# Twelve weight pieces of layer 1: the low part formed by a negation and an accumulating DMA in place of a subtraction on VectorE

## The chip, the cores and the metric

The kernel runs on one core of one Trainium2 chip. The metric is the device time of one execution in microseconds; the median of 3 runs of the kernel before is 1392.16 us (1390.02 to 1392.28).

## The reference

Two layers of a gated block on 512 tokens with 1024 channels, all in float32. What matters of it:

```python
for i in range(DEPTH):                                   # 2 layers
    xn = rmsnorm(x, norm1_g[i])
    proj = xn @ w_in[i]
    u_pool, q, k, v, g_a, g_b = jnp.split(proj, splits, axis=-1)
    ...                                                  # 4 heads, two q/k pairs of 128 each, v of 256
    q = apply_partial_rotary(rmsnorm(q, q_norm_g[i]), cos, sin)     # k the same
    o = diff_attention(q, k, v, lam)                     # softmax(q0 k0) - lam * softmax(q1 k1), chunk-causal, times v
    o = rmsnorm(o, subln_g[i]) * (1.0 - lam_init)
    pool_out = pool_mixer(u_pool, pool_w[i], pool_scale[i])
    merged = sigmoid(g_a) * pool_out + sigmoid(g_b) * o
    x = x + merged @ w_out[i]
    gate, up = jnp.split(rmsnorm(x, norm2_g[i]) @ w_ffn_in[i], 2, axis=-1)
    x = x + (silu(gate) * up) @ w_ffn_out[i]
```

## The kernel before

**Products in three parts.** Every float32 operand is split into a high part, rounded to the type that TensorE multiplies (fp32r), and a low part, the remainder. A product is then three matmuls into the same accumulator: high by high, high by low, low by high (`product`, `three`, `in_turn`; lines 271 to 273 and 290 to 292).

**Weights.** They come from HBM in 243 pieces of 128 x 1024 floats (512 KB, two rows of 128 channels by 512 columns) in the order of a list. `loaded` issues a piece's load on SyncE's queue into one of 7 `raw` buffers. `parts` makes its two parts in one of 6 pairs of buffers (`whi`, `wlo`). It has two forms:

- Without a piece number it calls `split` (line 201): ScalarE copies the piece into `whi`, and VectorE subtracts that from the piece into `wlo`.
- With a piece number (lines 225 to 227) ScalarE copies the piece into `whi` and writes the negated piece into `wlo` (an activation with scale -1), and GpSimd issues a DMA from the weights in HBM that adds the piece to `wlo` as it lands, so that the remainder is left. The DMA waits for the negation, and for this form a piece is read from HBM twice. 64 pieces take it, all of them in the feed-forward parts.

`wblock` gives the four pieces of one block of `w_in` for one head (1024 channels by 512 columns), all by the first form. A head has three such blocks: q/k, v with one gate, and u with the other gate.

**Order of the heads.** The heads are taken in the order 3, 2, 1, 0 (`ORDER`). `attention(j, before, then)` computes a head's q and k for four blocks of 128 tokens (each: 24 matmuls, an eviction with squares on ScalarE, the norm and the rotation on VectorE), then v and a gate. After q and k of the next head's second block, `then` computes the previous head's u and gate part (`merged`). The list of loads has the same order: q/k of a head, its v/gate, and then the u/gate of the head before.

**Work between the matmuls.** Scores, softmax, the product with v and the norm behind it are put into a heap with a due time (`later`), and taken out between the matmuls of other products when a count of TensorE's columns (`clock`) has passed it (`run_due`). So TensorE's order is: some weights' matmuls, then the scores of one block, and so on.

**Transposes through HBM.** In all heads but the first of layer 0, q and k, the probabilities and the attention's output are transposed by `turned` (lines 300 to 320): VectorE transposes in 32 x 32 squares into `near` (line 305), SyncE's queue writes `near` to HBM (`away`) and reads it back in four pieces (line 310). Then ScalarE casts the result to its high part (`qh`, or `ah` for the probabilities) and VectorE subtracts the low part (`ql`, `al`), both with line 201. Scores are lines 505 to 525, the casts and the product with v lines 538 to 558.

**GpSimd** does two things here: the power of -1/2 of the norms (`r`, line 335), in between VectorE's sums and its scaling (line 589), and the issuing of the accumulating DMAs (line 227), both in one queue in the order of the program. Also on ScalarE's queue is a DMA: the load of the pooling weights (`pwr`, line 638), into one of the same 7 `raw` buffers.

Of the kernel before, what the change touches and what calls it, by code (L numbers as in the profile page):

```python
# [23 lines left out]
KD = D // P  # L24
# [26 lines left out]
ORDER = (3, 2, 1, 0)  # L51
# [72 lines left out]
def trunk_kernel(  # L124
# [16 lines left out]
    def mm_ps():  # L141
        return ps.tile([P, 512], F32, name="mm", tag="mm", bufs=6)
# [60 lines left out]
    def split_half(hi, lo, src):  # L203

        half = nc.scalar.activation(hi, src, AF.Copy, scale=0.5)
        return half, nc.vector.scalar_tensor_tensor(lo, src, 0.5, hi.bitcast(F32), op0=ALU.mult, op1=ALU.subtract)

    def loaded():

        i = at[0]  # L210
        at[0] += 1
        raw = sb.tile([P, 2, 512], F32, name="raw", tag="raw", bufs=RAWS)
        transfers.append(nc.sync.dma_start(raw.rearrange("p a b -> p (a b)"), wts[i]))
        return raw, i
# [3 lines left out]
    def parts(raw, piece_no=None):  # L218

        hi = sb.tile([P, 2, 512], F32R, name="whi", tag="whi", bufs=SPLITS)  # L220
        lo = sb.tile([P, 2, 512], F32R, name="wlo", tag="wlo", bufs=SPLITS)
        if piece_no is None:
            made[:] = split(hi, lo, raw)
        else:
            nc.scalar.copy(hi, raw)
            made[0] = nc.scalar.activation(lo, raw, AF.Copy, scale=-1.0)  # L226
            nc.gpsimd.dma_start(lo.rearrange("p a b -> p (a b)"), wts[piece_no], accum_op=ALU.add)  # L227
        return hi, lo

    def rows_of(pair, n=2):  # L230

        hi, lo = (x.rearrange("p a b -> p (a b)").rearrange("p (k c) -> p k c", k=n) for x in pair)
        return [(hi[:, k, :], lo[:, k, :]) for k in range(n)]

    def piece(n=2, by_dma=False):
        raw, i = loaded()
        return rows_of(parts(raw, i if by_dma else None), n)

    def wblock(n):

        return [pair for _ in range(n // 2) for pair in piece()]


    clock = [0]
# [40 lines left out]
    def product(acc, pairs):  # L285

        n = len(pairs)
        for i, ((ah, al), (bh, bl)) in enumerate(pairs):
            run_due()
            nc.tensor.matmul(acc, lhsT=ah, rhs=bh, start=i == 0, stop=False)  # L290
            nc.tensor.matmul(acc, lhsT=ah, rhs=bl, start=False, stop=False)  # L291
            last = nc.tensor.matmul(acc, lhsT=al, rhs=bh, start=False, stop=i == n - 1)  # L292
            clock[0] += 3 * acc.shape[-1]
        return last
# [48 lines left out]
    def need(*keys):  # L343
        run_due(lambda: all(k in ready for k in keys))
# [9 lines left out]
    def pair(name, tag, n):  # L354
        return [sb.tile([P, n, S], F32R, name=name + part, tag=tag, bufs=2) for part in "hl"]
# [117 lines left out]
    for layer in range(L):  # L473
# [8 lines left out]
        def x_all(t0=0, t1=NT):  # L482
            return [(xh[:, k, t0 * P:t1 * P], xl[:, k, t0 * P:t1 * P]) for k in range(KD)]

        def cut(pairs, c0, c1):
            return [(h[:, c0:c1], l[:, c0:c1]) for h, l in pairs]

        def attention(j, before, then):

            if before is not None:  # L490
# [84 lines left out]

            at_start = not layer and j == ORDER[0]
            if not at_start:
                w = wblock(KD)
            held = []

            def evicted(t, acc):
# [33 lines left out]
                need(*((layer, before, "o", t) for t in range(NT)))  # L615
            vh, vl = pair("v", "v", 2)
            tb = [sb.tile([P, 2, VD], F32, name="tb", tag="tb", bufs=2) for _ in range(2)]
            w = wblock(KD)
            if at_start:
                with tc.issue_after(transfers[-1].ins):  # L620
                    for i in range(L):
# [14 lines left out]
        def pool_weights(j):  # L636
            raw = sb.tile([P, 2, VD], F32, name="pwr", tag="raw", bufs=RAWS)
            nc.scalar.dma_start(raw.rearrange("p a b -> p (a b)"), pool_w[layer, j])
            both = sb.tile([P, 2, 2, VD], F32R, name="pw", tag="pw")
            hi, lo = both[:, 0], both[:, 1]  # L640
            split(hi, lo, raw)
            return [(hi[:, a, :], lo[:, a, :]) for a in range(2)]

        def windowed(j, c, acc, uh, ul):

            window = WINDOWS[j]
            up = sb.tile([P, 16 + S], F32, name="up", tag="up", bufs=2)
            nc.vector.memset(up[:, :16], 0.0)
            nc.vector.tensor_mul(up[:, 16:], acc, rms_rows[layer])
            prev, step, n = up, 1, 0  # L650
            while step < window:
                cur = sb.tile([P, 16 + S], F32, name="us", tag="us", bufs=2)
                nc.vector.memset(cur[:, :16], 0.0)
                nc.vector.tensor_add(cur[:, 16:], prev[:, 16:], prev[:, 16 - step:16 + S - step])
                prev, step, n = cur, step * 2, n + 1
            head = sb.tile([P, 16], F32, name="head", tag="head", bufs=2)
            nc.vector.tensor_mul(head, prev[:, 16:32], inv_t[:, j, :])
            nc.vector.scalar_tensor_tensor(
                prev[:, 32:], prev[:, 32:], 1.0 / window, up[:, 32:], op0=ALU.mult, op1=ALU.subtract)
            nc.vector.tensor_sub(prev[:, 16:32], head, up[:, 16:32])  # L660
            split(uh[:, c, :], ul[:, c, :], prev[:, 16:])

        def merged(j, mj, mh, ml):

            w = wblock(KD)
            pw = pool_weights(j)
            uh, ul = pair("u", "u", 2)
            for c in range(2):
                acc = mm_ps()
                product(acc, list(zip(cut(w, c * P, (c + 1) * P), x_all())))  # L670
                windowed(j, c, acc, uh, ul)

            gates = []
            for c in range(2):
                acc = mm_ps()
                product(acc, list(zip(cut(w, VD + c * P, VD + (c + 1) * P), x_all())))
                ta = sb.tile([P, S], F32, name="ta", tag="ta", bufs=2)
                nc.vector.tensor_mul(ta, acc, rms_rows[layer])
                nc.scalar.activation(ta, ta, AF.Tanh, scale=0.5)
                gates.append(ta)  # L680
            need(*((layer, j, "mj", t) for t in range(NT)))
            for c in range(2):
                y = mm_ps()
                product(y, list(zip(cut(pw, c * P, (c + 1) * P), [(uh[:, a, :], ul[:, a, :]) for a in range(2)])))
                ta = gates[c]
                k = KD * layer + 2 * j + c
                nc.vector.scalar_tensor_tensor(ta, ta, 1.0, y, op0=ALU.add, op1=ALU.mult)
                nc.vector.scalar_tensor_tensor(ta, ta, scale[:, k:k + 1], mj[:, c, :], op0=ALU.mult, op1=ALU.add)
                split_half(mh[:, c, :], ml[:, c, :], ta)
# [257 lines left out]
        def mix(i):  # L947
            j = ORDER[i]
            if i == 2:
                need(*((layer, ORDER[3], "s", t) for t in range(NT)))  # L950
                ms[j] = pair("m", "qk", 4)
            else:
                ms[j] = pair("m", "m", 2)
            merged(j, mjs[j], *ms[j])

        for i, j in enumerate(ORDER):
            then = (lambda: project_out(ORDER[i - 2])) if i >= 2 else None
            mjs[j] = attention(j, ORDER[i - 1] if i else None, then)
            if i:
                mix(i - 1)  # L960
# [68 lines left out]
```

## Time and profile before

| | |
|---|---|
| median of 3 runs | 1392.16 us (1392.28, 1390.02, 1392.16) |
| profiled execution, its own time | 1391.49 us |
| its span in the profile | 1389.7 us |
| TensorE busy | 1375.8 us, 99% |
| VectorE busy | 1042.5 us, 75% |
| ScalarE busy | 704.1 us, 51% |
| GpSimd busy | 118.2 us, 9% |
| mean granted TensorE clock | 0.997 |
| weight pieces made by an accumulating DMA | 64 of 243 |

How to read it: the span is the time between the first and the last instruction that the profiler saw; the execution's own time is 1.8 us longer. Layer 1 begins at about 690 us in this profile. A line such as L201 is line 201 of the kernel; PE is TensorE, DVE VectorE, ACT ScalarE, POOL GpSimd, SP SyncE. In a timeline each row has the start in us, the length in us, the engine, the line, the operation, output<-inputs, and in brackets the idle time before it and what ended it.

### The profile page before, as it was taken

How to read it: one execution, taken by the hardware profiler on the slowest of the kernel's cores; microseconds unless marked ns; L12 is line 12 of the kernel's file. 1: busy time of each engine (PE TensorE's matmuls, PEld its weight loads, DVE VectorE, ACT ScalarE, POOL GpSimd, SP SyncE). 2: the span in 40 equal slices, each digit the busy share in tenths (PEclk: the TensorE clock that was granted, in tenths of full speed). 3: DMA queues.
4: the chain of work that ended last, by engine and by line, in shares of the span. 5: the costliest groups of instructions: out<-in, count | busy, mean ns of one | idle time of the engine just before them, and what ended most of it. 6: DMA issues, size and time to landing. Idle time of an engine off the chain costs nothing.

```text
span 1389.7 us, 18568 instructions
## 1 busy us (share of the span) xinstructions
PE 1375.8 (99%) x6242; PEld 1142.0 (82%) x6242; DVE 1042.5 (75%) x1979; ACT 704.1 (51%) x1321; POOL 118.2 (9%) x139
## 2 busy tenths in 40 slices
PE   9999999999999999999999889999999999999999
PEld 7888888888888888888888778888888888888887
DVE  7778778786869768578667787786868686785782
ACT  7545353454766545564435443444547565554540
POOL 1010100000111001110011100000001010011100
PEclk9999999999999999999999999999999999999999
DMA  8333454444667868686334345534446688687741
GB/s 311 104 124 112 147 162 131 148 136 134 152 181 191 240 177 225 164 208 209 109 121 137 106 135 165 163 122 148 140 129 151 183 199 220 195 219 173 199 129 61
DMA packets 141071, 224.52 MB, mean 162 GB/s; under 512 B 40880, under 2 KB 88496, under 8 KB 140976
## 3 DMA queue, kind: packets, MB, share of 16 engines
q1 hardware_dynamic: 130464, 187.65, 42.1%
q0 software_dynamic: 9216, 33.56, 13.8%
q10 hardware_dynamic: 1296, 2.12, 0.5%
q8 instruction: 49, 0.80, 0.2%
q14 instruction: 46, 0.38, 0.1%
HBM read 194.04 MB, written 29.23 MB: 161 GB/s over the span
## 4 chain that ended last, share of the span: by engine, by line
PE 93%; DVE 3%; issue 1%; DMA 1%; POOL 1%; ACT 0%; SPq 0%; DVEq 0%; POOLq 0%; ACTq 0%
PE mm L272 14%; PE mm L273 14%; PE mm L271 14%; PE mm L292 13%; PE mm L290 13%; PE mm L291 13%; PE sc L271 3%; PE sc L273 3%; PE sc L272 3%; PE sc L291 1%; PE sc L292 1%; PE sc L290 1%; DVE qn L589 1%; POOL r L335 1%; DVE wlo L201 1%
## 5 line engine op out<-in xcount | busy, mean ns | idle before, releaser
L201 DVE TENSOR_TENSOR wlo<-raw,whi 128x1024 fp32r<-128x1024 f32 (+1 forms) x221 | 266.7, 1211 | 62.9 <-ACT whi L201 62.3
L201 ACT CAST whi<-raw 128x1024 fp32r<-128x1024 f32 (+1 forms) x221 | 229.9, 1047 | 165.0 <-PE mm L273 60.3
L290 PE MATMUL mm<-whi,xh 128*128 128x512 f32 x480 | 189.0, 394 | 0.0
L291 PE MATMUL mm<-wlo,xh 128*128 128x512 f32 x480 | 187.5, 391 | 0.0
L292 PE MATMUL mm<-whi,xl 128*128 128x512 f32 x480 | 187.3, 390 | 0.0
L273 PE MATMUL mm<-fh,wlo 128*128 128x512 f32 (+1 forms) x356 | 137.8, 387 | 0.0
L272 PE MATMUL mm<-fl,whi 128*128 128x512 f32 (+1 forms) x356 | 137.8, 387 | 0.0
L271 PE MATMUL mm<-fh,whi 128*128 128x512 f32 (+1 forms) x356 | 137.8, 387 | 0.0
L692 DVE TENSOR_TENSOR res<-mm,res 128x512 f32<-128x512 f32 (+1 forms) x145 | 98.1, 680 | 43.1 <-PE mm L273 41.8
L292 PEld LDWEIGHTS mm<-whi,xl 128*128 128x128 f32 x480 | 90.3, 188 | 19.2
L290 PEld LDWEIGHTS mm<-whi,xh 128*128 128x128 f32 x480 | 90.4, 188 | 17.4
L291 PEld LDWEIGHTS mm<-wlo,xh 128*128 128x128 f32 x480 | 90.5, 188 | 17.2
L227 POOL DMA_DIRECT2D wlo<-in_wts x64 | 56.1, 877 | 536.8 <-ACT wlo L226 364.1
L335 POOL TENSOR_TENSOR r<-r,mhalf 128x1 f32<-128x1 f32 (+1 forms) x64 | 56.4, 882 | 528.8 <-DVE r L334 509.0
L291 PE MATMUL mm<-xl,whi 128*128 128x512 f32 x256 | 100.4, 392 | 0.0
L290 PE MATMUL mm<-xh,whi 128*128 128x512 f32 x256 | 100.3, 392 | 0.0
L292 PE MATMUL mm<-xh,wlo 128*128 128x512 f32 x256 | 100.0, 391 | 0.0
L273 PE MATMUL mm<-whi,xl 128*128 128x512 f32 x224 | 87.2, 389 | 0.0
L271 PE MATMUL mm<-whi,xh 128*128 128x512 f32 x224 | 87.2, 389 | 0.0
L272 PE MATMUL mm<-wlo,xh 128*128 128x512 f32 x224 | 87.2, 389 | 0.0
L226 ACT ACTIVATE wlo<-raw 128x1024 fp32r<-128x1024 f32 x64 | 67.7, 1057 | 29.0 <-PE mm L272 27.3
L271 PEld LDWEIGHTS mm<-fh,whi 128*128 128x128 f32 x356 | 66.9, 188 | 13.6
(217 smaller groups left out, 2939.4 us busy)
## 6 DMA issues: line engine op xcount, KB each, us to landing
raw<-in_wts SPq DMA_DIRECT2D x243, 512.0 KB, 3.9
wlo<-in_wts POOLq DMA_DIRECT2D x64, 512.0 KB, 6.1
away<-near SPq DMA_DIRECT2D x72, 256.0 KB, 2.4
near<-away SPq DMA_DIRECT2D x288, 64.0 KB, 2.5
away<-near SPq DMA_DIRECT2D x28, 128.0 KB, 1.7
near<-away SPq DMA_DIRECT2D x112, 32.0 KB, 2.5
pwr<-in_pool_w ACTq DMA_DIRECT2D x8, 256.0 KB, 2.7
away<-pr SPq DMA_DIRECT2D x7, 256.0 KB, 2.0
```

The source lines that it names most:

```text
L201: return nc.scalar.copy(hi, src), nc.vector.tensor_sub(lo, src, hi.bitcast(F32))
L226: made[0] = nc.scalar.activation(lo, raw, AF.Copy, scale=-1.0)
L227: nc.gpsimd.dma_start(lo.rearrange("p a b -> p (a b)"), wts[piece_no], accum_op=ALU.add)
L271: nc.tensor.matmul(acc, lhsT=ah, rhs=bh, start=start, stop=False, **check)
L272: nc.tensor.matmul(acc, lhsT=ah, rhs=bl, start=False, stop=False, **check)
L273: last = nc.tensor.matmul(acc, lhsT=al, rhs=bh, start=False, stop=stop, **check)
L290: nc.tensor.matmul(acc, lhsT=ah, rhs=bh, start=i == 0, stop=False)
L291: nc.tensor.matmul(acc, lhsT=ah, rhs=bl, start=False, stop=False)
L292: last = nc.tensor.matmul(acc, lhsT=al, rhs=bh, start=False, stop=i == n - 1)
L335: nc.gpsimd.tensor_tensor(r, r, mhalf[:, :width], op=ALU.pow)
L589: nc.vector.scalar_tensor_tensor(qn[:, h, :], acc[:, h * QK:(h + 1) * QK], r[:, h:h + 1], g, op0=ALU.mult, op1=ALU.mult)
L692: return nc.vector.tensor_add(res[d][:, cs], acc, res[d][:, cs])
```

## The change

`wblock` takes a number of pieces that are to be made by the second form. In layer 1, for the first two heads of the order (3 and 2), and for each of their three blocks, that is two of four: the first two pieces. So twelve pieces, two heads by three blocks by two, are made by a copy and a negation on ScalarE and an accumulating DMA that GpSimd issues, where they were made by a copy on ScalarE and a subtraction on VectorE. Nothing else is changed in the code.

```diff
-    def wblock(n):
-
-        return [pair for _ in range(n // 2) for pair in piece()]
+    def wblock(n, by_dma=0):
+
+        return [pair for i in range(n // 2) for pair in piece(2, i < by_dma)]
...
+        def by_dma(j):
+            return 2 if layer and j in ORDER[:2] else 0
+
         def attention(j, before, then):
...
-                w = wblock(KD)
+                w = wblock(KD, by_dma(j))
...
             tb = [sb.tile([P, 2, VD], F32, name="tb", tag="tb", bufs=2) for _ in range(2)]
-            w = wblock(KD)
+            w = wblock(KD, by_dma(j))
...
         def merged(j, mj, mh, ml):

-            w = wblock(KD)
+            w = wblock(KD, by_dma(j))
```

The compiler's scheduler places the instructions on each engine by the costs that it assumes, so the order changes as well. Lines behind line 487 have numbers that are larger by 3 in the changed kernel. Three places:

VectorE at head 3's third block of q and k, in layer 1: `r` is the norm's factor, `qn` the scaled q and k, `m` the rotation, `wlo` the weights of head 2's q/k block, `ql` the low part of an earlier block, and `near` the square transpose that begins the trip through HBM. Before:

```order
L334 TENSOR_SCALAR r<-ss_6696,stats 128x2 x2
L589 SCALAR_TENSOR_TENSOR qn<-mm,r,hg 128x128 x4
L201 TENSOR_TENSOR wlo<-raw,whi 128x1024
L362 TENSOR_TENSOR m_6709<-qn,tab 128x128
L366 TENSOR_TENSOR m_6709<-qn,tab 128x4x16 x2
L201 TENSOR_TENSOR wlo<-raw,whi 128x1024
L367 TENSOR_TENSOR qn<-m_6709 128x4x32
L201 TENSOR_TENSOR ql<-near,qh 128x4x128
L201 TENSOR_TENSOR wlo<-raw,whi 128x1024
L305 STREAM_TRANSPOSE near<-qn 128x4x4x32
```

And now:

```order
L334 TENSOR_SCALAR r<-ss_6698,stats 128x2 x2
L592 SCALAR_TENSOR_TENSOR qn<-mm,r,hg 128x128 x4
L201 TENSOR_TENSOR wlo<-raw,whi 128x1024
L362 TENSOR_TENSOR m_6711<-qn,tab 128x128
L366 TENSOR_TENSOR m_6711<-qn,tab 128x4x16 x2
L201 TENSOR_TENSOR ql<-near,qh 128x4x128
L367 TENSOR_TENSOR qn<-m_6711 128x4x32
L305 STREAM_TRANSPOSE near<-qn 128x4x4x32
```

The two subtractions on either side of `qn` and `ql` are gone, and `ql` stands one place earlier.

ScalarE where head 3's scores of its third block (`pr`, 384 columns) are made and head 2's v/gate weights are split; `vh` and `tb` are evictions of head 3's v and gate, `pwr` is the load of the pooling weights. Before:

```order
L201 CAST whi<-raw 128x1024 x2
L627 ACTIVATE vh<-mm,stats 128x256
L201 CAST whi<-raw 128x1024
L201 CAST ah<-pr 128x128
L630 ACTIVATE tb<-mm,stats 128x256
L520 ACTIVATE pr,st<-sc,mx 128x384 x2
L638 DMA pwr<-in_pool_w 128x512
```

And now:

```order
L201 CAST whi<-raw 128x1024
L225 CAST whi<-raw 128x1024
L226 ACTIVATE wlo<-raw 128x1024
L630 ACTIVATE vh<-mm,stats 128x256
L201 CAST ah<-pr 128x128
L225 CAST whi<-raw 128x1024
L523 ACTIVATE pr,st<-sc,mx 128x384 x2
L633 ACTIVATE tb<-mm,stats 128x256
L226 ACTIVATE wlo<-raw 128x1024
L641 DMA pwr<-in_pool_w 128x512
```

Two negations have come in, one of them directly ahead of the load of `pwr`, and `tb` stands behind `pr` now.

GpSimd from the end of layer 0 through the heads of layer 1; the rows with a minus are before, those with a plus now, and `r` is the power of the norms:

```order
-L227 DMA wlo<-in_wts 128x1024 x26
+L227 DMA wlo<-in_wts 128x1024 x30
 L416 TENSOR_TENSOR stats<-stats,mhalf 128x4
-L335 TENSOR_TENSOR r<-r,mhalf 128x4 x6
+L335 TENSOR_TENSOR r<-r,mhalf 128x4 x3
+L227 DMA wlo<-in_wts 128x1024 x2
+L335 TENSOR_TENSOR r<-r,mhalf 128x4
+L227 DMA wlo<-in_wts 128x1024 x2
+L335 TENSOR_TENSOR r<-r,mhalf 128x4 x2
```

Four of the twelve issues stand before layer 1's first norm of q and k, and of the next four two stand ahead of the power for head 3's fourth block, two ahead of those for head 2's first and second block.

TensorE's order is the same but for two matmuls of head 2's first q/k block, which stand behind the six matmuls of head 3's last scores (512 columns) instead of ahead of them.

## The prediction

> **What bounds the kernel now.** I read the page first: the engines' shares, and the DMA queues.
>
> ```profile
> PE 1375.8 (99%) x6242; PEld 1142.0 (82%) x6242; DVE 1042.5 (75%) x1979; ACT 704.1 (51%) x1321; POOL 118.2 (9%) x139
> ...
> q1 hardware_dynamic: 130464, 187.65, 42.1%
> q0 software_dynamic: 9216, 33.56, 13.8%
> ```
>
> TensorE is busy for 1375.8 of 1389.7 us. VectorE, which the change relieves, has a quarter of its time free. So a subtraction less is worth something only where TensorE waits for VectorE, and all of TensorE's idle time is 1389.7 - 1375.8 = 13.9 us. The waits of TensorE say where the largest pieces are:
>
> ```profile
> PE mm L290 <- ACT ah L201: 6.4, 2, 3.2
> PE sc L290 <- ACT pr L520: 0.9, 1, 0.9
> ```
>
> The columns are the total, the count and the longest. TensorE's timeline then dates the waits in layer 1's first heads (the bracket is the idle time before the row, and what ended it):
>
> ```profile
> 732.39 0.39 PE L290 MATMUL sc<-qh 128*128 128x256 f32 x1 [0.86 <-ACT pr L520]
> 769.60 0.39 PE L290 MATMUL mm<-vh,ah 128*128 128x256 f32 x1 [3.24 <-ACT ah L201]
> 790.91 0.44 PE L291 MATMUL sc<-ql,qh 128*128 128x384 f32 x1 [0.54 <-DVE ql L201]
> 820.61 0.39 PE L290 MATMUL mm<-vh,ah 128*128 128x256 f32 x1 [3.15 <-ACT ah L201]
> 821.51 0.39 PE L292 MATMUL mm<-vh,al 128*128 128x256 f32 x1 [0.40 <-DVE up L648]
> ```
>
> I number them: stall 0 (0.86), stall 1 (3.24), stall 2 (0.54), stall 3 (3.15 and 0.40), 8.19 us together. The windows behind stalls 1 and 3 show a second loss. The column after POOL is the granted clock:
>
> ```profile
> 770.60:774.00 3.40, 3.34 (x13) 2.96 (x13) 3.37 (x5) 0.00 (x0) 0.00 (x0) 0.50 0.15 48
> 821.60:825.10 3.50, 3.50 (x13) 3.01 (x14) 1.43 (x5) 0.51 (x3) 0.54 (x1) 0.53 0.55 142
> ```
>
> At half clock, 3.4 us of work take the place of 1.7, so each spell loses about 1.7 us. With 8.2 + 3.4 = 11.6 us the most that this stage can give back is 0.8% of the time. Everything depends on which stalls the removed subtractions stand in front of.
>
> The row behind stall 3 has the clock at 0.53 after a gap of 3.15 us. "TensorE: Matmul & The Clock Gate" of the Trainium skill (Part 1, on the HAM clock gate) lets the clock fall to one half after an idle window of about 3.4 us, in windows that run free of the program. The trace differs in the figure: gaps of 3.24 and 3.15 us were enough here.
>
> **The change part by part.** Twelve weight pieces (4 each for q/k, v/gate and u/gate, in two heads' worth: 2 x 3 x 2) change from a VectorE subtraction to a ScalarE negation plus an accumulating DMA. The prices of one of each:
>
> ```profile
> L201 DVE TENSOR_TENSOR wlo<-raw,whi 128x1024 fp32r<-128x1024 f32 (+1 forms) x221 | 266.7, 1211 | 62.9 <-ACT whi L201 62.3
> ...
> L227 POOL DMA_DIRECT2D wlo<-in_wts x64 | 56.1, 877 | 536.8 <-ACT wlo L226 364.1
> ...
> L226 ACT ACTIVATE wlo<-raw 128x1024 fp32r<-128x1024 f32 x64 | 67.7, 1057 | 29.0 <-PE mm L272 27.3
> ...
> wlo<-in_wts POOLq DMA_DIRECT2D x64, 512.0 KB, 6.1
> ```
>
> VectorE loses 12 x 1.21 = 14.5 us; ScalarE gains 12 x 1.06 = 12.7 us; GpSimd 12 x 0.88 = 10.5 us of issuing. Of the DMA engines, the 64 accumulating transfers on q0 took 13.8% of 1389.7 us, which is 3.0 us of all sixteen engines for each, so 36 us more. These are sums beside TensorE; what counts is their place. Four of the twelve (head 3's q/k and v/gate) are formed before 705 us, where TensorE doesn't wait; two (head 2's u/gate) lie behind 830 us, where it doesn't wait either. I cost these six at nothing: what hides them is the stretch of matmuls with no gap around them, and a landing of 6.1 us that is late by 1 or 2 us would show as a gap of that size. Six are left: head 2's q/k at 719 to 722 us, its v/gate at 738 to 744, head 3's u/gate at 771 to 773.
>
> *Stall 0, head 2's q/k pieces.* The chain of waits that ends at 732.39, in order of time (start, length, what):
>
> ```profile
> 719.06 0.27 DVE m L366 x2
> 719.33 0.10 DVE wlo L201
> ...
> 720.38 0.29 DVE qn L367
> 720.67 0.60 DVE ql L201
> 721.27 1.14 DVE wlo L201
> 722.41 0.63 DVE near L305
> 723.04 0.02 issue
> 723.05 2.15 DMA away<-near
> ...
> 726.60 3.04 DMA near<-away
> ...
> 729.96 0.61 ACT qh L201
> ...
> 730.59 1.28 ACT L520
> ...
> 731.88 0.47 ACT pr L520 x2
> ```
>
> Both subtractions in it go. From the end of m at 719.33, qn (0.29) and ql (0.60) then lead to near at about 720.3, so the round trip through HBM starts 2.1 us earlier. Against that, the two accumulating DMAs are issued at about 718 and 721 (I place them behind the negations on ScalarE), so up to 6.0 us of sixteen engines fall where the engines are needed for the trip and the raw loads. Before, the DMA share (the column before the last) is this:
>
> ```profile
> 724.00:726.00 2.00, 2.00 (x11) 1.65 (x10) 0.58 (x3) 1.08 (x4) 1.01 (x1) 1.00 1.01 300
> 726.00:728.00 2.00, 2.00 (x10) 1.66 (x9) 2.00 (x9) 0.80 (x2) 0.00 (x0) 1.00 0.99 375
> ```
>
> The engines are full there already. The trip (723.05 to 729.64, 6.6 us) grows by nothing at the least and by 3.0 us, one accumulating transfer, at the most. So qh comes 2.1 us earlier to 0.9 later, and stall 0 becomes 0 to 1.8. I take a trip 1.5 us longer, the middle, since the windows show no free share to hide more: qh 0.6 earlier, stall 0 at 0.26, a gain of 0.6 us. The page "DMA: Bandwidth & Descriptors" of the Trainium skill (Queues, rings and completion order) says that each DMA engine takes turns between the queues it has work for, packet by packet. By that alone the trip's two transfers (2.15 and 3.04 us) could take twice as long beside the accumulating ones, 5.2 us more, and stall 0 would be an estimated 4.0 us, 3.1 longer than now, and the sum 1395.2; the trace has no accumulating transfer beside a trip, so no run so far shows it.
>
> *Scores of the largest blocks, head 2's v/gate pieces.* The ScalarE and VectorE rows around them:
>
> ```profile
> 743.98 0.33 ACTq L638 DMA_DIRECT2D pwr<-in_pool_w  x1
> ...
> 749.92 0.62 ACT L201 CAST pw<-pwr 128x512 fp32r<-128x512 f32 x1 [1.11 <-DMA pwr<-in_pool_w]
> ```
>
> ```profile
> 742.72 1.22 DVE L201 TENSOR_TENSOR wlo<-raw,whi 128x1024 fp32r<-128x1024 f32 x1
> ...
> 751.30 0.68 DVE L201 TENSOR_TENSOR pw<-pwr,pw 128x512 fp32r<-128x512 f32 x1
> ```
>
> Two negations (2.1 us) now stand on ScalarE ahead of or between the work that frees TensorE's score banks, and two subtractions less on VectorE make that work ready earlier; the two nearly cancel. TensorE's rows there are these:
>
> ```profile
> 743.85 0.39 PE L292 MATMUL mm<-whi,xl 128*128 128x512 f32 x1
> 744.07 0.39 PE L290 MATMUL sc<-qh 128*128 128x512 f32 x1
> ```
>
> Two such weight matmuls, 0.22 us apart, now stand behind the six score matmuls, so TensorE reaches the scores 0.45 us earlier and may wait there: 0 to 0.6, I take 0.3. The load of pwr goes into a buffer that a subtraction freed at 743.94 (742.72 + 1.22) and now the second negation frees, by my count of ScalarE's queue at 745.8, 1.9 later. It landed 1.11 us after ScalarE was ready for it. VectorE's pw at 751.30 stood a little behind it (749.92 + 0.62 = 750.54, so 0.8 us of slack), so it can be 1.1 us late, and it stands in VectorE's queue ahead of the rotation of head 2's first block. What that delays is the chain toward stall 1: 0 to 1.4 us. I take 0.3, near the lower end, since that chain waits next for TensorE's own product.
>
> *Stall 1, head 3's u/gate pieces.* ScalarE and VectorE before it:
>
> ```profile
> 766.10 2.92 ACT L201 CAST whi<-raw 128x1024 fp32r<-128x1024 f32 x3
> 768.93 0.62 ACT L201 CAST ah<-pr 128x512 fp32r<-128x512 f32 x1
> ```
>
> ```profile
> 770.14 0.69 DVE L201 TENSOR_TENSOR al<-pr,ah 128x512 fp32r<-128x512 f32 x1
> 770.74 2.35 DVE L201 TENSOR_TENSOR wlo<-raw,whi 128x1024 fp32r<-128x1024 f32 x2
> ```
>
> What TensorE waits for (ah) is behind three casts on ScalarE, and these three casts stay, since the high part of a piece is cast in both forms; the two new negations come behind ah. The two removed subtractions start at 770.74, after the wait has ended at 769.60. So stall 1 keeps its 3.24 us, and its half clock. Stalls 2 and 3 have no removed subtraction between TensorE's preceding product and themselves, and I cost them at nothing, between 0.5 gained (stall 2 gone, since 2.35 us of VectorE go at 770.74) and 0.5 lost.
>
> The sum: 1391.5 (the profiled execution's own time) - 0.6 + 0.3 + 0.3 = 1391.5. That execution is 0.7 below the median of the runs, 1392.16; the median moves by the same nothing. I put the forecast at 1392.0, between the two.
>
> **The rivals.**
>
> *A, slower: the accumulating DMAs crowd the round trip.* The trip of head 3's third block grows by the full 3.0 us, stall 0 becomes 0.86 + 0.9 = 1.8, and a wait of that size brings a spell of half clock (1.7 us). With the 0.3 at the scores that is 2.9, so 1395.1. For it: the DMA share of 1.01 and 0.99. Against it: the start is 2.1 us earlier, and only from a trip longer by more than 2.1 us does it cost anything; a gap of 0.86 us brought no half clock.
>
> *B, faster: the relief reaches the long stalls.* If VectorE carries a backlog from 719 us on, 14.5 us less of it bring ah forward at stalls 1 and 3. Shortened by a quarter each (1.6 us), they no longer bring half clock (3.4 us): 1392.0 - 5.0 = 1387.0. For it: ah needs pr, which VectorE makes. Against it: ah stood behind ScalarE's casts, and TensorE's products start the chains anew.
>
> *C, about the same by another way: the clock alone.* A spell comes or goes by the place of a gap in time, at 1.7 us each: 1390.3 or 1393.7. The gaps of 3.24 and 3.15 us are near enough to each other to be one case, and the one of 0.86 us is far off, so this has little for it. The page on the clock gate (Part 1) has windows that run free of the program, by which a shift of 1 or 2 us alone could do it.
>
> That the change doesn't do what it says is ruled out by the order of the instructions: VectorE has 12 rows fewer, and GpSimd and ScalarE have the 12 issues and negations more.
>
> **How the numbers follow.** A measurement of this kernel can tell about 0.2% from no change, 2.8 us: below 1389.4 is faster, above 1394.9 slower. Chances: my forecast 0.57, A 0.20, B 0.13, C 0.10. B is faster, with 0.02 for a C of two spells: 0.15. A is slower: 0.20. The rest is 0.65. The range reaches from 1389.0, which leaves out most of B, to 1395.3, which holds A's price and leaves out what is beyond it: about 0.1 below and 0.08 above.
>
> **What would show it.** In the profile after: near of the third block at about 720.3 instead of 722.41 and its trip longer by 0 to 3 us; stall 0 at 0 to 0.9; the two 3 us waits for ah at their places with 0.50 beside them; pw about 1 us later; no waits for wlo as a DMA's work. I am wrong if a wait of over 1 us appears at a wlo of the twelve, or a wait on GpSimd's queue (its rsqrt stands in the same queue as the new issues, which wait for negations), or if the waits for ah shrink by more than 1 us.

## The result and the profile after

The changed kernel takes 1400.42 us (median of 4 runs, 1399.7 to 1400.98) against 1391.82 us for the kernel before (4 runs): a ratio of 1.0064, 95% interval 1.0047 to 1.0081, slower by 8.6 us. The forecast was 1392.0 us with a range from 1389.0 to 1395.3.

The profiled execution has a span of 1399.1 us, 9.4 more than before. The page's engine shares and the two large DMA queues:

```profile
PE 1379.7 (99%) x6242; PEld 1142.6 (82%) x6242; DVE 1029.2 (74%) x1967; ACT 714.8 (51%) x1333; POOL 129.1 (9%) x151
...
q1 hardware_dynamic: 130464, 187.65, 42.2%
q0 software_dynamic: 10944, 39.85, 16.2%
```

The change did what it says: VectorE has 12 instructions and 13.3 us less, ScalarE and GpSimd some 11 us more, and q0 carries twelve more transfers (39.85 against 33.56 MB). TensorE has the same 6242 matmuls, but is busy for 3.9 us longer and idle for 5.5 us longer. TensorE's waits say which waits grew:

```profile
PE mm L290 <- ACT ah L201: 6.6, 3, 3.1
PE sc L290 <- ACT pr L523: 3.9, 1, 3.9
PE mm L292 <- DVE al L201: 2.6, 3, 1.5
```

The two waits for ah of 3 us each are still there. Stall 0 is 3.9 us where it was 0.9, and the waits for al come to 2.6 us where they came to 0.3: two of the three are new. The chain of waits that ends at stall 0 (start, length, what), to be held against the chain shown in the prediction:

```profile
720.82 0.73 DVE near L305
...
721.57 8.67 DMA away<-near
...
731.62 1.97 DMA near<-away
...
733.68 0.62 ACT qh L201
...
734.32 1.28 ACT L523
...
736.12 0.58 PE sc L290
```

near stands 1.6 us earlier than before, and 2.2 against the work around it, since this execution was already 0.65 us later when it came to layer 1's heads. That part of the forecast came true. But the write of near to HBM takes 8.67 us where it took 2.15. The round trip (721.57 to 733.60) is 12.0 us where it was 6.6, so qh comes 3.7 us later and not 0.6 earlier. The windows over the write, with the DMA share in the column before the last and GB/s in the last:

```profile
724.00:726.00 2.00, 2.00 (x11) 1.65 (x10) 1.81 (x8) 0.26 (x1) 0.16 (x1) 1.00 1.01 225
726.00:728.00 2.00, 2.00 (x11) 1.65 (x10) 0.48 (x4) 0.88 (x3) 0.00 (x0) 1.00 1.10 273
...
736.00:738.00 2.00, 1.88 (x8) 1.78 (x9) 1.11 (x6) 1.07 (x5) 0.00 (x0) 0.50 0.29 79
738.00:740.00 2.00, 2.00 (x6) 1.61 (x5) 0.70 (x4) 0.88 (x4) 0.00 (x0) 0.50 0.11 33
740.00:742.00 2.00, 2.00 (x7) 1.57 (x7) 1.13 (x4) 1.07 (x4) 0.00 (x0) 0.65 0.13 20
```

The engines were full at 724 to 728 us before as well (1.01 and 0.99), but moved 300 and 375 GB/s then, and 225 and 273 now. Behind the stall, the column after POOL shows a third spell of half clock, 736.1 to 741.4: 5.3 us of work at half speed, 2.6 us lost (1.88 x 0.5 + 2.0 x 0.5 + 2.0 x 0.35).

The second loss is at the load of pwr. ScalarE's rows there, then TensorE's:

```profile
751.73 0.33 ACTq L641 DMA_DIRECT2D pwr<-in_pool_w  x1
...
759.77 0.62 ACT L201 CAST pw<-pwr 128x512 fp32r<-128x512 f32 x1 [4.56 <-DMA pwr<-in_pool_w]
```

```profile
763.02 0.39 PE L292 MATMUL mm<-vh,al 128*128 128x256 f32 x1 [1.52 <-DVE al L201]
...
778.01 0.39 PE L290 MATMUL mm<-vh,ah 128*128 128x256 f32 x1 [2.95 <-ACT ah L201]
```

pwr takes 8.0 us to land (5.9 before), ScalarE waits 4.56 us for it (1.11 before), and the casts and subtractions queued behind it on ScalarE and VectorE are late: TensorE waits 0.48 us for ah and 1.52 us for al. Stall 1 then is 0.3 us shorter.

So of the 9.4 us: stall 0 +3.1, its half clock +2.6, pwr +2.0, stall 1 -0.3, a wait for al near 925 us +0.8, whose cause no run shows, and 0.65 that lay ahead of layer 1's heads (in the kernel without the transfers, below, the same place is 1.0 us later than before, so this isn't theirs). That leaves some 0.6 us that I don't assign.

### The profile page after: what moved, and what is told of

It reads as the page before. It is cut to its first block, busy times and chain, and to the rows that moved or that the text cites. A ratio compares the mean times of both kernels' runs of the same rounds, so it can differ in the third digit from the quotient of the medians.

```text
span 1399.1 us, 18602 instructions
## 1 busy us (share of the span) xinstructions
PE 1379.7 (99%) x6242; PEld 1142.6 (82%) x6242; DVE 1029.2 (74%) x1967; ACT 714.8 (51%) x1333; POOL 129.1 (9%) x151
## 3 DMA queue, kind: packets, MB, share of 16 engines
q0 software_dynamic: 10944, 39.85, 16.2%
q10 hardware_dynamic: 1296, 2.12, 0.5%
## 4 chain that ended last, share of the span: by engine, by line
PE 86%; DVE 5%; DMA 3%; ACT 2%; issue 2%; SPq 1%; POOL 1%; ACTq 0%; DVEq 0%; POOLq 0%
PE mm L272 14%; PE mm L271 14%; PE mm L273 14%; PE mm L292 11%; PE mm L290 11%; PE mm L291 11%; PE sc L271 3%; PE sc L273 3%; PE sc L272 3%; DMA away<-pr 1%; SPq L310 1%; POOL r L335 1%; DVE qn L592 1%; DMA away<-near 1%; DVE wlo L201 1%
## 5 line engine op out<-in xcount | busy, mean ns | idle before, releaser
L201 DVE TENSOR_TENSOR wlo<-raw,whi 128x1024 fp32r<-128x1024 f32 (+1 forms) x209 | 252.3, 1211 | 62.3 <-ACT whi L201 61.7
L201 ACT CAST whi<-raw 128x1024 fp32r<-128x1024 f32 (+1 forms) x209 | 217.5, 1046 | 155.8 <-PE mm L273 61.5
L227 POOL DMA_DIRECT2D wlo<-in_wts x76 | 66.8, 879 | 653.3 <-ACT wlo L226 449.9
L226 ACT ACTIVATE wlo<-raw 128x1024 fp32r<-128x1024 f32 x76 | 80.3, 1058 | 29.0 <-PE mm L272 25.7
L225 ACT CAST whi<-raw 128x1024 fp32r<-128x1024 f32 x76 | 79.1, 1042 | 21.2 <-issue 15.3
```

Of the source, the lines that this page charges most:

```text
L201: return nc.scalar.copy(hi, src), nc.vector.tensor_sub(lo, src, hi.bitcast(F32))
```

## The experiments

Two theories stood at first. **Crowding**: the accumulating transfers hold the DMA engines just when the round trips and pwr need them. **Queues**: the negations on ScalarE, the issues in GpSimd's queue and the new order of the instructions make things late. Medians are in us; differences are between medians, and ratios are to the kernel before, run beside.

**The transfers left out.**

```diff
-            nc.gpsimd.dma_start(lo..., wts[piece_no], accum_op=ALU.add)
+            if not apart:       # apart: the twelve pieces
+                nc.gpsimd.dma_start(lo..., wts[piece_no], accum_op=ALU.add)
```

> The changed kernel with the twelve accumulating DMAs left out (the copy, the negation on ScalarE and the missing subtraction stay, so the low parts of twelve pieces hold the negated weights). Theory 'crowding' (the transfers hold the DMA engines while SyncE's trips and the load of pwr need them): the write of near before stall 0 is back at 2 to 3 us from 8.67, stall 0 is 0 to 0.9 us, the waits for ah and al at 761 to 763 us (0.48 and 1.52) are gone, and the time is 1390 to 1392. Rival 'queues' (the negations on ScalarE and the new order of the instructions are what is late): stall 0 stays above 2 us and the time at 1397 or more.

1391.20 (10 runs) against 1391.65, ratio 0.9995 (0.9986 to 1.0005). The write of near takes 2.7 us, and stall 0 is gone altogether; what is left in TensorE's waits:

```profile
PE mm L291 <- ACT ah L201: 6.4, 2, 3.2
...
PE sc L292 <- DVE ql L201: 0.5, 1, 0.5
```

All negations and the new order are in this kernel, and it loses nothing. Of what 'queues' names it lacks the twelve issues on GpSimd, which went with the transfers; the kernel with plain transfers below has them and loses nothing either, so queues fell. The run also gives what the change could have gained: with its transfers free, 0.45 us, not clear of zero, and by the interval at most 2 us.

**Head 2's q/k pieces alone, and all the others.** A block's name is now given to `by_dma`:

```diff
-            return 2 if layer and j in ORDER[:2] else 0
+            return 2 if layer and (b, j) in (("qk", 2),) else 0
```

> Only the two pieces of head 2's q/k block by accumulating DMA, the other ten by subtraction. 'Crowding': the two transfers at 718 to 730 us alone give stall 0 of 3 to 4 us and a spell of half clock behind it (some 2.7 us), no waits for al at 763: 1391.8 + 3.1 + 2.7 = 1397.6. 'Queues': the loss is spread over the twelve, two give at most a third of it, under 1395.

1397.13, ratio 1.0036 (1.0023 to 1.0049): +5.5. The write of near in its chain, and stall 0:

```profile
720.95 8.86 DMA away<-near
```

```profile
735.76 0.58 PE L290 MATMUL sc<-qh 128*128 128x256 f32 x1 [4.17 <-ACT pr L523]
```

> The ten other pieces by accumulating DMA, head 2's two q/k pieces by subtraction. 'Crowding': stall 0 is that of before, 0.9 us, with no half clock behind it; pwr is late still, so the waits for ah and al (2.0 us) and the one near 925 us (0.8) stay: 1391.8 + 2.8 = 1394.6. 'Queues': five sixths of the loss stay, 1399.

1395.77, ratio 1.0028 (1.0018 to 1.0039): +4.1, where 2.8 was expected (the wait near 925 us is 1.16 here, and stall 0 is 1.11). The trip is back, and the wait for al behind pwr is there:

```profile
723.10 2.18 DMA away<-near
...
726.67 3.48 DMA near<-away
```

```profile
757.24 0.39 PE L292 MATMUL mm<-vh,al 128*128 128x256 f32 x1 [1.51 <-DVE al L201]
```

Two of the twelve pieces cost about as much as the other ten, since the intervals overlap: place counts, not number. (5.5 + 4.1 is 1.0 more than the whole; the intervals of the two, 1.8 and 1.5 us to either side, cover it.)

**Plain transfers in place of accumulating ones.**

```diff
-            nc.gpsimd.dma_start(lo..., wts[piece_no], accum_op=ALU.add)
+            if apart:
+                nc.gpsimd.dma_start(lo..., wts[piece_no])
+            else:
+                nc.gpsimd.dma_start(lo..., wts[piece_no], accum_op=ALU.add)
```

> The changed kernel with the twelve transfers plain instead of accumulating: the same bytes from the same place at the same time, written over the negated weights (the low parts then hold the weights themselves). If it is the accumulation that makes a transfer dear (3.0 us of all sixteen engines by the first trace, against 1.6 for a plain load of 512 KB), the write of near takes some 5 us, stall 0 is 0.5 to 1.5 us without half clock, and the time 1393 to 1395. If the bytes alone count, or the turns between queues, all stays: 1400.

1392.04, ratio 1.0003 (0.9994 to 1.0013), under the 1393 to 1395 expected. The write of near takes 4.18 us, and stall 0 is 0.85 again:

```profile
720.93 4.18 DMA away<-near
```

```profile
732.41 0.39 PE L293 MATMUL sc<-qh 128*128 128x256 f32 x1 [0.85 <-ACT pr L526]
```

The trip starts 2.1 us earlier than in the kernel before and takes 2.3 us longer, and the two cancel. pwr lands in 5.0 us, and no wait for al stands behind it. The twelve issues stand in GpSimd's queue as in the changed kernel, at 0.5 to 0.6 us each in place of 0.9. The DMA rows of 721 to 730 us show what differs; the columns are packets, MB and the share of sixteen engines. The changed kernel:

```profile
q0 software_dynamic: 283, 1.05, 60.9%
q1 hardware_dynamic: 894, 1.17, 39.8%
```

And with plain transfers:

```profile
q1 hardware_dynamic: 1728, 2.12, 67.4%
q0 software_dynamic: 288, 1.05, 35.9%
```

The same 1.05 MB on q0 takes 60.9% of 9 us in accumulating form and 35.9% in plain form, so 2.7 and 1.6 us of all sixteen engines for each of the two transfers. And q1, with the raw loads and the trip, moves 1.17 MB in that time beside the one and 2.12 MB beside the other. So the loss comes with the accumulation. The same bytes on the same queue without it lengthen the write too, by 2.0 us, but the trip by no more than the earlier start gives back. The two queues' shares add up to the whole in both kernels (60.9 and 39.8, 35.9 and 67.4): what the accumulating transfers take more, the hardware queue has less.

**Head 2's v/gate pieces alone, and the eight others.** The same edit, with `("vg", 2)`, and with q/k, v/gate and u/gate of head 3 and u/gate of head 2.

> Only the two pieces of head 2's v/gate block by accumulating DMA. 'Crowding': the load of pwr takes some 8 us to land, as in the changed kernel (8.0), against 5.9 before, and the waits for ah and al in front of it (some 0.5 and 1.5 us) come, stall 0 stays at 0.9; no new half clock; 1391.7 + 2.0 = 1393.7. Rival 'the buffer' (pwr is late because its raw buffer is freed by the negation, about 2 us later than by the subtraction): the same time, but pwr's transfer itself takes under 6 us.

1394.21, ratio 1.0018 (1.0008 to 1.0027): +2.3. pwr's eight loads, where before the longest was 5.9:

```profile
DMA to landing us min/median/max: 2.5/2.7/8.2
```

So pwr's transfer itself is slow beside the accumulating ones; a later buffer alone would have left it under 6. The kernel without the transfers shows the later buffer by itself: pwr is issued at 745.58 us there (745.46 here, 743.98 before), none of its loads takes more than 3.2 us, and no wait comes of it.

> The eight other pieces by accumulating DMA: head 3's three blocks and head 2's u/gate; head 2's q/k and v/gate by subtraction. 'Crowding': neither stall 0 nor the waits at 761 to 763 us; only the late wait for al near 925 us (0.8 to 1.2) is left if head 2's u/gate makes it: 1392.5, within 0.2% of before. 'Queues': two thirds of the loss, 1397.

1392.70, ratio 1.0008 (0.9998 to 1.0017): +0.8. The wait near 925 us is 0.32 here. The parts add up: 5.5 + 2.3 + 0.8 = 8.6, the whole loss. (The ten pieces in one kernel cost 4.1, these two groups 3.1; the intervals cover that.)

**One piece, and four.** `return 1` and `return 4` for head 2's q/k block.

> Only one piece of head 2's q/k block by accumulating DMA. 'Crowding', half the traffic: the trip is longer by about half of the 5.4 us of the changed kernel, 2.7, its start earlier by about 1.2; stall 0 is 0.86 + 1.5 = 2.4 us. If a stall of that size brings half clock, 1391.7 + 1.5 + 1.7 = 1394.9, if not 1393.2.

1392.32, ratio 1.0003 (0.9994 to 1.0013). The write of near takes 6.14 us. The write, stall 0, and the window behind it with the full clock:

```profile
721.26 6.14 DMA away<-near
```

```profile
733.88 0.39 PE L290 MATMUL sc<-qh 128*128 128x256 f32 x1 [2.01 <-ACT pr L523]
```

```profile
734.00:736.00 2.00, 2.00 (x12) 1.78 (x13) 1.74 (x9) 1.40 (x6) 0.00 (x0) 1.00 0.12 36
```

A stall of 2.01 us brought no half clock, so the second transfer costs more than the first: it takes the stall from 2.0 to 4.2 and adds the spell.

> All four pieces of head 2's q/k block by accumulating DMA (with one, the write of near took 6.1 us and stall 0 was 2.0; with two 8.9 and 4.2). 'Crowding', in proportion: some 3 us of the sixteen engines for each further piece, and the third block's trip starts no earlier, so stall 0 is 6 to 10 us, as far as the third and fourth transfers are issued before the trip is over; 1400 to 1404. If the third and fourth come behind the trip, stall 0 stays at 4 us, and the next trip is late instead.

1401.06, ratio 1.0067 (1.0051 to 1.0084). The third and fourth transfer came 22 us behind the first two, so stall 0 is 3.5, and TensorE waits for one of them, a wait that neither branch of the expectation had:

```profile
PE mm L291 <- DMA wlo<-in_wts: 4.0, 1, 4.0
```

A spell of half clock stands behind each of the two.

**The two transfers behind the trip.** GpSimd must first have read the cast qh of the third block:

```diff
+                late = sb.tile([P, 1], F32, name="late", tag="r", bufs=4)
+                turned_qh = behind[:, 0, 2 * P:2 * P + 1].bitcast(F32)
+                nc.gpsimd.tensor_tensor(late, turned_qh, turned_qh, op=ALU.subtract)
+                nc.gpsimd.tensor_tensor(lo[:, 0, :1], lo[:, 0, :1].bitcast(F32), late, op=ALU.add)
             nc.gpsimd.dma_start(lo..., wts[piece_no], accum_op=ALU.add)
```

> As the run with head 2's q/k pieces alone, but GpSimd issues the two transfers only behind the cast qh of head 3's third block (it adds a zero worked out from qh to one column of the low part ahead of each issue). The negations, the missing subtractions and the bytes are the same. 'Crowding': the trip is over when the transfers start, so stall 0 is 0 to 0.3 us, no half clock, and the time 1391 to 1392.5, unless the later landing (some 738 to 742 us) makes TensorE wait for a low part at 741. If it isn't the place in time of the transfers, 1397 as there.

1397.71 (4 runs, 1394.85 to 1398.79), ratio 1.0040 (1.0025 to 1.0055). Stall 0 is gone, as expected, but the time isn't back. The transfers start at 731 to 733 us and meet the next trip, that of the first probabilities. SyncE's queue (the read at 739.72 waits for the write at 733.27):

```profile
733.27 0.34 SPq L312 DMA_DIRECT2D away<-pr  x1
739.72 1.73 SPq L316 DMA_DIRECT2D pr<-away  x4
```

A write of 64 KB takes 6.4 us, against a median of 1.8 us in the changed kernel. ScalarE waits for the trip, and pr stands behind that cast in its queue:

```profile
742.97 0.30 ACT L201 CAST ah<-pr 128x128 fp32r<-128x128 f32 x1 [3.40 <-DMA pr<-away]
```

TensorE's waits then, and windows behind them:

```profile
745.20 0.80 PE L296 MATMUL sc<-qh 128*128 128x512 f32 x1 [3.15 <-ACT pr L531]
...
773.24 0.39 PE L296 MATMUL mm<-vh,ah 128*128 128x256 f32 x1 [3.12 <-ACT ah L201]
```

```profile
746.00:748.00 2.00, 2.00 (x6) 1.54 (x6) 0.67 (x4) 0.07 (x1) 0.00 (x0) 0.50 0.74 200
...
773.00:777.00 4.00, 3.67 (x21) 2.98 (x22) 4.00 (x5) 0.71 (x2) 0.00 (x0) 1.00 0.24 66
```

This profiled execution is the fastest of the four, 1394.85 us at a mean granted clock of 0.998; the others, 2.4 to 3.9 us slower, have 0.995. The wait at 773 us brought no half clock here; that the others lost their time to more of it is likely, but no trace of them shows it. My expectation was wrong: it had only one trip in view. The theory stands, since the wait went where the transfers went.

**The long wait itself.** As the change never reached stall 1, I tried what stands in front of it, in the kernel before:

```diff
-            w = wblock(KD)
+            w = wblock(KD, nc.gpsimd.tensor_copy if layer and j == ORDER[0] else None)
```

> The kernel before, with no new transfers; the high parts of head 3's four u/gate pieces in layer 1 are copied by GpSimd in place of ScalarE. The long wait for ah near 770 us (3.2 us, and its half clock 1.7) stands behind ScalarE's casts of three pieces, by the traces; with one cast left ahead of it, ah comes 2 us earlier: 1391.8 - 2 = 1389.8, or 1388 if the half clock goes as well. Rival: GpSimd's copies take several us each and stand in its queue ahead of the norms' powers, and the subtractions wait for them, so al is late in place of ah: 1392 to 1396.

1394.23, ratio 1.0018 (1.0009 to 1.0028): slower. ah comes earlier, and al later by more:

```profile
768.39 0.39 PE L290 MATMUL mm<-vh,ah 128*128 128x256 f32 x1 [1.35 <-ACT ah L201]
...
772.82 0.58 PE L292 MATMUL mm<-vh,al 128*128 128x256 f32 x1 [3.01 <-DVE al L201]
```

GpSimd's first two copies, and two of VectorE's rows ahead of al in that time:

```profile
768.67 2.08 POOL L201 CAST whi<-raw 128x1024 fp32r<-128x1024 f32 x2
```

```profile
769.16 0.70 DVE L367 TENSOR_TENSOR qn<-m 128x128 f32<-128x128 f32 x1
769.78 1.25 DVE L558 SCALAR_TENSOR_TENSOR mt<-tb,mt 128x256 f32<-128x256 f32 x1
```

The copies take 1.0 us each here, not several. In the kernel before, the two VectorE rows take 0.28 and 0.42 us; the 1.25 us that they take more here are the whole delay of al beyond the 0.7 us by which this execution was late already. So al is late as the rival said, but the trace shows slower rows on VectorE there, and no wait of a subtraction for the copies.

No run points to a version that beats the kernel before.

## Why the prediction was wrong

- **What bounds the kernel, and what the relief is worth: right.** The most to be had was put at the stalls of layer 1, and the removed subtractions stood in front of stall 0 only, for a gain of 0.6 us. The kernel without the transfers shows 0.45 us, and the trip did start 2.2 us earlier against the work around it, for 2.1 forecast.
- **The step that failed is the length of the trip at stall 0.** The prediction put its growth at "nothing at the least and by 3.0 us, one accumulating transfer, at the most", and took 1.5. It was 5.4 (12.0 against 6.6). Two transfers were in flight beside it, issued at 719.05 and 721.47 us against a write at 721.57, and I priced one. The bound had no reason behind it: the prediction's own figures put both issues at about 718 and 721, 6.1 us from landing, with 6.0 us of all sixteen engines for the two. And it was too low even for one: one alone lengthened the write of near by 4.0 us (6.14 against 2.15) and the trip by 3.5, two the write by 6.5.
- **The half clock belonged to that bound.** I gave rival A 1.7 us of half clock at a stall of 1.8. A stall of 2.01 us, with one piece, brought none, so that condition was wrong; the stall was 3.9 and the spell 5.3 us long, so 2.6. Rival A was the mechanism, with the size too small: 2.6 of its 2.9 us are for these two pieces, and 5.5 were measured with them alone.
- **The estimate worked out from the Trainium skill came near by luck.** From "DMA: Bandwidth & Descriptors" of the Trainium skill (Queues, rings and completion order) came an estimated stall of 4.0 us; 3.9 and 4.2 were measured. The estimate doubles both transfers of the trip, the write from 2.15 and the read from 3.04. Beside the accumulating transfers the write took four times as long (8.67), and the read, behind them, less than before (1.97); beside plain ones the write did about double (4.18), the read took 3.29, and the stall stayed at 0.85. So turns between queues fit the plain transfers' write, and not what happened in the changed kernel.
- **pwr: right mechanism, wrong size.** I took 0.3 us of 0 to 1.4; it cost 2.0, for the same reason: its transfer grew by 2 us (8.0 against 5.9), and I had counted the later buffer alone, at 1.9 us. That buffer came 1.5 us later with head 2's v/gate pieces alone, and in the kernel without the transfers it cost nothing.
- **Eight pieces costed at nothing**, six of them as hidden: not contradicted, +0.8 with an interval that reaches to no change.
- **Stalls 1, 2 and 3 unmoved: right** (2.95, 0.58, 3.15 and 0.41 against 3.24, 0.54, 3.15 and 0.40). Rival B was never near.
- **Rival C is in the noise, not in the 8.6 us.** The 25 runs of the kernel before beside the second group of experiments go from 1390.03 to 1393.63 us, and their times go with the clock: two at a mean granted clock of 0.999 average 1390.2 us, seven at 0.998 1391.0, twelve at 0.997 1392.0, four at 0.996 1393.0.

What stays open is why an accumulating transfer takes 1.7 times the engines' time of a plain one. That the other queue is slowed goes with the shares that add up to the whole.

## What to carry to other kernels

A transfer that replaces arithmetic is paid for in the DMA engines, in the few microseconds in which it is in flight: look for a latency-bound round trip in that window before you look at the busy shares of the compute engines, and count every transfer that can be in flight with it. A plain and an accumulating transfer of the same bytes are not the same price. And before adding cost elsewhere to relieve an engine, run the kernel with the relief alone: here it was worth 0.45 us, and by the interval at most 2.

## What the runs showed of the hardware

- 512 KB accumulated from HBM into SBUF took 2.7 us of all sixteen DMA engines, plain 1.6, and beside the accumulating pair the hardware queue moved 1.17 MB in 9 us instead of 2.12.
- A gap on TensorE of 0.86, 1.52 or 2.01 us left the clock at 1.00; gaps of 2.65 (in the run with GpSimd's copies), 2.95, 3.15, 3.94 and 4.17 us brought half clock. One of 3.12 us, in the run with the delayed transfers, did not, while one of 3.15 us in the same execution did. So near 3 us the length alone doesn't decide: a shorter gap brought half clock and a longer one didn't. "TensorE: Matmul & The Clock Gate" of the Trainium skill (Part 1) has windows that run free of the program, which agrees with that; its figure of about 3.4 us of idle time is more than what was enough here.
- Beside two copies of 128x1024 on GpSimd (2.08 us), two operations on VectorE took 0.70 and 1.25 us that took 0.28 and 0.42 without them.
